# A hybrid decoder layer on one core: softmax scalings and a convolution step moved to ScalarE, norms of the last product by ScalarE, third tile by an accumulating store

## The chip, the cores and the metric

The kernel runs on one core of a Trainium2 chip. A core has a matrix engine (PE, TensorE), three engines for elementwise work (DVE = VectorE, ACT = ScalarE, POOL = GpSimd) and a queue engine, SP, that mainly issues transfers (DMAs). Each engine has its own queue of instructions, which it works through strictly in order; semaphores order the engines among each other. Transfers are issued from SP, from ACT and from POOL. The metric is the device time of one execution in microseconds (us), the median over several runs. The profile is of one execution.

## The reference

One layer of a hybrid decoder on 1,024 tokens of width 1,024, with 16 learned tokens put in front (1,040 rows), everything in 32-bit floating point:

```python
u = rmsnorm(h, g_pre_mix)
q, k, v, xr, yr = split(u @ w_in)                 # 512, 128, 128, 512, 512 columns
attn = sliding_window_attention_with_sinks(q, k, v, sinks)   # 8 heads of 64, 2 KV heads
xr = causal_depthwise_conv(xr, conv_w, conv_b)    # width 4
hr = rg_lru(xr, w_a, b_a, w_x, b_x, lru_lambda)   # sigmoid gates, exp, sqrt, scan over time
rec = gelu(yr) * hr
h = h + rmsnorm(concat(attn, rec) @ w_out, g_post_mix)
u = rmsnorm(h, g_pre_ffn)
f = square(relu(u @ w_ff1)) @ w_ff2               # 4096 hidden columns
return (h + rmsnorm(f, g_post_ffn))[16:]
```

An rmsnorm divides each row by the root of its mean square plus 1e-6 and multiplies by a gain per column. The softmax divides by the sum of the exponentials and of exp(sink - maximum).

## The kernel before, in words

**Matrix products.** A 32-bit operand is split into a rounded high part and the remainder (`split`, lines 93 to 100: a cast on ACT at line 95, a subtraction on DVE at line 98), and each product is three matmuls (`mm3`, lines 122 to 125: high by high, high by low, low by high). Both feed-forward products are done with seven half-size products in place of eight (a Strassen scheme), so sums of weight blocks and of activation blocks are made on the way, on DVE (`combine`, line 788) or by an accumulating DMA, which adds what it loads to what is there and is issued by POOL.

**Buffers.** Nearly all tiles come from rings named by tag: "raw" 2 slots, "ws" 4, "a" 16, "b" 17, "c" 8, "d" 4, "e" 2. A slot is given to a new tile when all that read the old tile is done, so a tag also settles when a load may start.

**Order.** The program is written stage by stage; a scheduler of the tile framework, which uses its own model of the machine's times, orders the instructions of each engine. Hand-made order edges come on top: `lut` (line 81) chains all table functions of ACT in the order in which they are written, and `behind` puts DVE work behind a given instruction.

**Stages**, with the times of the profiled execution: loading, norm and transposes to about 24 us. Attention to about 230 us: for four head pairs and two halves `scores` computes the scores, takes maxima (line 467, DVE), exponentials (Exp, ACT), reciprocals of the sums and scales the eight 128x256 blocks by them (line 480, DVE); `attend`, one group later, transposes the scaled blocks on PE (line 495), splits them and multiplies with the values. Between groups PE gets "fills": the projections of queries, of the recurrent branch and of its gate. A projected recurrent chunk goes through `conv` (first step at line 530: multiply by the last tap and add the bias; three more steps on DVE). Then, to about 285 us, the gates (sigmoids), decay and recurrence (Exp, Tanh, Sqrt, a scan on DVE, line 650), the Gelus (`rec_out`), and the output projection (`out_mm`, eight slices of its contraction; the first four, from attention, don't need the recurrent branch). ACT works through the sigmoids, four Exp/Tanh and two Sqrt groups and eight Gelus, for which it loads another function table each time, and through casts of w_out slices among them. Then the first feed-forward product to about 580 us and the second to 964 us, in seven passes `(i, q)` of eight steps each.

**The second product.** `fetch_2` loads the weights of a step four to six steps ahead: a first operand, and for most steps a second one, either by an accumulating DMA or into a slot of its own, which `combine` then adds or subtracts. Tags alternate between "raw" and "e"; for the last pass `LASTW` lists them. `evict` adds the passes' results into accumulators. Output tiles 4 to 7 are complete after pass 5 (`finish_early`), tiles 0 to 3 after pass 6: `finish_half` takes the sum of squares of the columns that are done, `finish_late` the rest. The rows of `out` hold h already. Tiles 0 and 1 (and 4 to 7) are added to it by an accumulating store of POOL; for tiles 2 and 3 h is loaded back (line 1143 and after), added on DVE (line 1177), and stored by SP and ACT, half each (line 1180). The factor of a norm is the power -1/2 of mean square plus 1e-6, computed by POOL (`rstd_of`, line 164; line 1173).

Of the kernel before, what the change touches and what calls it, by code (L numbers as in the profile page):

```python
# [9 lines left out]
F32 = mybir.dt.float32  # L10
F32R = mybir.dt.float32r
AF = mybir.ActivationFunctionType
ALU = mybir.AluOpType
# [3 lines left out]
P = 128  # L17
# [10 lines left out]
EPS = 1e-6  # L28
# [9 lines left out]
def hybrid_layer(  # L38
# [6 lines left out]
    nc = tc.nc  # L45
# [109 lines left out]
    def rstd_of(ssq_parts, n=P):  # L155
        ms = small.tile([P, 1], F32, name="ms", tag="ms")
        if len(ssq_parts) == 1:
            nc.gpsimd.tensor_scalar(ms[:n], ssq_parts[0], EPS, None, op0=ALU.add)
        else:
            nc.vector.scalar_tensor_tensor(  # L160
                ms[:n], ssq_parts[0], EPS, ssq_parts[1], op0=ALU.add, op1=ALU.add
            )
        rs = small.tile([P, 1], F32, name="rs", tag="rs")
        nc.gpsimd.tensor_tensor(rs[:n], ms[:n], half_pow[:n], op=ALU.pow)  # L164
        return rs[:n]


# [264 lines left out]
    def scores(j, half, q):  # L432
        sn = [slot("c", [P, 4, 257]) for _ in range(2)]
        negm = small.tile([P, 2, 4], F32, name="negm", tag="negm")
        den = small.tile([P, 2, 4], F32, name="den", tag="den")
        rden = small.tile([P, 2, 4], F32, name="rden", tag="rden")
        for h in range(2):
            nc.vector.tensor_copy(
                sn[h][:, :, 256], nsink[:, j + 4 * h : j + 4 * h + 1].to_broadcast([P, 4])
            )  # L440
        for bp in range(2):
            for h in range(2):
                sp_ = bank("s", (P, 2, 256))

                def qk(dst, b, hi, lo):
                    c = slice(b * P, (b + 1) * P)
                    nc.tensor.matmul(
                        dst, q[h][:, c], hi, start=True, stop=False,
                        skip_group_check=True,
                    )  # L450
                    nc.tensor.matmul(
                        dst, q[h][:, c], lo, start=False, stop=True,
                        skip_group_check=True,
                    )

                for i in range(2):
                    b = 4 * half + 2 * bp + i
                    if b == 0:
                        qk(sp_[:, i, 0:P], b, km[:, h, :], km[:, 2 + h, :])
                        qk(sp_[:, i, P:256], b, khh[h][:, 0:P], kl[h][:, 0:P])  # L460
                    else:
                        c = slice((b - 1) * P, (b + 1) * P)
                        qk(sp_[:, i, :], b, khh[h][:, c], kl[h][:, c])
                for i in range(2):
                    b = 4 * half + 2 * bp + i
                    k = 2 * bp + i
                    nc.vector.tensor_tensor_reduce(
                        out=sn[h][:, k, 0:256], in0=sp_[:, i, :],
                        in1=mask1 if b == 0 else mask, scale=-1.0,
                        scalar=nsink[:, j + 4 * h : j + 4 * h + 1],  # L470
                        op0=ALU.add, op1=ALU.min, accum_out=negm[:, h, k : k + 1],
                    )
                    lut(
                        sn[h][:, k, :], sn[h][:, k, :], AF.Exp, scale=-1.0,
                        bias=negm[:, h, k : k + 1], accum_out=den[:, h, k : k + 1],
                    )
        for h in range(2):
            nc.vector.reciprocal(rden[:, h, :], den[:, h, :])
            for k in range(4):
                nc.vector.tensor_scalar(  # L480
                    sn[h][:, k, 0:256], sn[h][:, k, 0:256], rden[:, h, k : k + 1],
                    None, op0=ALU.mult,
                )
        return sn

    def attend(j, half, sn):
# [40 lines left out]

    def conv(c, xr, tag="d"):
        y = slot(tag, [P, TT])
        nc.vector.tensor_scalar(  # L530
            y, xr, prm[:, c, 3:4], prm[:, c, 4:5], op0=ALU.mult, op1=ALU.add
        )
        for k in (2, 1, 0):
            s = 3 - k
            nc.vector.scalar_tensor_tensor(
                y[:, s:], xr[:, : TT - s], prm[:, c, k : k + 1], y[:, s:],
                op0=ALU.mult, op1=ALU.add,
            )
        xc[c] = y
# [247 lines left out]
    def combine(dst, x0, x1, op):  # L787
        return nc.vector.tensor_tensor(dst, x0, x1, op=op).ins  # L788
# [113 lines left out]
    for t in range(8):  # L902
# [12 lines left out]
        if t == 6:  # L915
            b21 = operand(u2f[0][2:4])
            hl = slot("b", ESH, F32R), slot("e", ESH, F32R)
            a11_early.update(early(0, 2, hl))

    for p in range(2):  # L920
        p1(p, a11_early[p])
    for p in range(2):
# [93 lines left out]
    def product_by_parts(acc, w, op):  # L1016
# [22 lines left out]


    LASTW = [
        ("raw", None), ("e", "raw"), ("b", None), ("b", None), ("raw", "e"), ("b", None),
        ("e", "raw"), ("b", None),
    ]

    def fetch_2(n):
        i, q = steps[n]
        wx = PLAN[i][1]
        tags = (("raw", "e"), ("e", "raw"))[n % 2] if i < 6 else LASTW[q]
        raws = []  # L1050
        for (a, b), tag in zip(wx[:2], tags):
            if len(wx) == 3 and wx[2] is ADD and raws and (
                q % 3 < 2 if i < 6 else tag is None
            ):
                nc.gpsimd.dma_start(raws[0], w2v[q, a, b], accum_op=ADD)
                break
            r = slot(tag, [P, 2, 512])
            nc.sync.dma_start(r, w2v[q, a, b])
            raws.append(r)
        return raws  # L1060
# [24 lines left out]
    w_low = [None]  # L1085
# [29 lines left out]
    def squares(sq, src, n):  # L1115
        p_ = small.tile([P, 1], F32, name=f"sq{n}", tag=f"sq{n}")
        nc.scalar.activation(sq, src, AF.Square, scale=RMS_SC, accum_out=p_)
        return p_

    def finish_early(j):  # L1120
        acc = facc["1", j]
        o = slot("a", [P, D])
        ssq = [squares(o[:, c], acc[:, c], n) for n, c in enumerate(COLS)]
        nc.vector.scalar_tensor_tensor(
            o, acc, rstd_of(ssq), gffn_b, op0=ALU.mult, op1=ALU.mult
        )
        t = 4 + j
        nc.gpsimd.dma_start(out[t * P : (t + 1) * P, :], o, accum_op=ALU.add)
# [3 lines left out]
    def finish_half(j):  # L1132

        o = slot("a", [P, D])
        acc, c = facc["0", j], COLS[1]
        ssq = small.tile([P, 1], F32, name=f"late{j}", tag=f"late{j}", bufs=1)
        nc.scalar.activation(
            o[:, c], acc[:, c], AF.Square, scale=RMS_SC, accum_out=ssq
        )
        h = None  # L1140
        if j > 1:
            h = slot("d", [P, D])
            nc.sync.dma_start(h, out[j * P : (j + 1) * P, :])
            nc.gpsimd.tensor_scalar(ssq, ssq, EPS, None, op0=ALU.add)
            behind(w_low[0], combine(o[:, c], acc[:, c], gffn_b[:, c], ALU.mult))
        halves[j] = h, o, ssq

    def finish_late(j, y, parts):

        h, o, ssq = halves[j]  # L1150
        acc = facc["0", j]
        for k, c in enumerate(parts):
            yield k
            ins = combine(acc[:, c], y[k], acc[:, c], ALU.add)
            if k == 1:
                behind(w_low[0], ins)
            if j < 2:
                w_low[0] = nc.vector.scalar_tensor_tensor(
                    o, acc, rstd_of([squares(o[:, c], acc[:, c], 0), ssq]), gffn_b,
                    op0=ALU.mult, op1=ALU.mult,  # L1160
                ).ins.name
                nc.gpsimd.dma_start(out[j * P : (j + 1) * P, :], o, accum_op=ALU.add)
                continue
            part = small.tile([P, 1], F32, name=f"part{k}", tag=f"part{k}")
            nc.vector.tensor_tensor_reduce(
                out=o[:, c], in0=acc[:, c], in1=acc[:, c], scale=RMS_SC * RMS_SC,
                scalar=ssq, op0=ALU.mult, op1=ALU.add, accum_out=part,
            )
            ssq = part
        if j < 2:  # L1170
            return
        rs = small.tile([P, 1], F32, name="rs", tag="rs")
        nc.gpsimd.tensor_tensor(rs, ssq, half_pow, op=ALU.pow)
        c = COLS[0]
        combine(o[:, c], acc[:, c], gffn_b[:, c], ALU.mult)
        for c, eng in zip(COLS[::-1], (nc.sync, nc.scalar)):
            w_low[0] = nc.vector.scalar_tensor_tensor(
                o[:, c], o[:, c], rs, h[:, c], op0=ALU.mult, op1=ALU.add
            ).ins.name
            eng.dma_start(out[j * P : (j + 1) * P, c], o[:, c])  # L1180
# [101 lines left out]
```

## Time and profile before

| | |
|---|---|
| median of 3 runs | 974.02 us (973.7 to 976.03) |
| profiled execution: time, span | 972.95 us, 971.1 us |
| PE busy, first to last matmul | 953.7 us, 5.8 to 964.0 us |
| DVE, ACT, POOL busy | 674.6, 502.0, 82.4 us |
| DMA, mean rate | 134 GB/s |
| granted clock of PE | 0.999 |
| DVE scaling 128x256 (L480), ACT Exp 128x257 | 0.350, 0.506 us |
| ACT cast 128x1024 (L95), DVE subtraction 128x1024 (L98) | 1.05, 1.22 us |
| ACT table load | 1.283 us each, 6 at L82 |
| POOL's pow, 128x1 (L164, L1173) | 0.57 (median of the late ones), 0.99 us |
| accumulating stores (L1162, L1128), issue to landing | 5.0 to 5.1, 6.5 to 9.8 us |
| plain half-tile stores (L1180), issue to landing | 2.1 to 2.6 us |

A busy time is the sum of an engine's instructions; successive instructions of ACT and DVE overlap by about 0.1 us, so what a series takes is less than the sum of its durations. For a single instruction the duration counts, for a series the distance from start to start. Matmuls of 512 columns start 0.23 us apart, those of 256 columns 0.12. In a timeline line the first number is the start, the second the duration, then engine, line of the code, operation, the tile written and the tiles read, and in brackets how long the engine stood idle before and what ended that.

### The profile page before, as it was taken

The numbers are of one execution on the slowest core, as the hardware profiler recorded it, in microseconds if no ns is written. First come the engines' busy times: TensorE is split into PE (matmuls) and PEld (weight loads), VectorE is DVE, ScalarE is ACT, GpSimd is POOL, SyncE is SP. The second block draws the span as 40 slices with busy tenths as digits, with TensorE's granted clock in tenths as the row PEclk, the third lists the DMA queues.
The fourth block names the chain that finished last, engine by engine and source line by source line (L and its number), as shares of the span: only waits on it lengthen the run. The fifth ranks groups of instructions, "written<-read, shape, count | busy, mean of one in ns | idle before, by whom it ended". The sixth has DMA issues, their size and how long they took to land.

```text
span 971.1 us, 12490 instructions
## 1 busy us (share of the span) xinstructions
PE 953.7 (98%) x4782; PEld 803.0 (83%) x4782; DVE 674.6 (69%) x997; ACT 502.0 (52%) x809; POOL 82.4 (8%) x109
## 2 busy tenths in 40 slices
PE   6999999999999999999999999999999999999997
PEld 6999999888878887888888878888888888888786
DVE  6679997775976686665645465468557676779694
ACT  6646673567844554343555556555433344445350
POOL 4100000000002100000000000000111000003152
PEclk9999999999999999999999999999999999999999
DMA  9002001012234466576522264323678765548923
GB/s 296 23 1 66 23 23 44 23 48 64 84 119 144 159 207 209 173 251 209 198 87 87 97 206 125 114 87 114 172 176 198 186 224 187 184 163 195 223 80 87
DMA packets 88219, 130.13 MB, mean 134 GB/s; under 512 B 13624, under 2 KB 52552, under 8 KB 88160
## 3 DMA queue, kind: packets, MB, share of 16 engines
q1 hardware_dynamic: 79792, 107.33, 33.4%
q0 software_dynamic: 7792, 20.45, 10.1%
q10 hardware_dynamic: 576, 1.57, 0.4%
q8 instruction: 37, 0.61, 0.2%
q14 instruction: 22, 0.18, 0.1%
HBM read 110.46 MB, written 18.87 MB: 133 GB/s over the span
## 4 chain that ended last, share of the span: by engine, by line
PE 89%; DVE 4%; DMA 3%; issue 2%; ACT 1%; POOL 0%; SPq 0%; POOLq 0%; DVEq 0%; ACTq 0%
PE ps_acc L124 11%; PE ps_acc L123 11%; PE ps_acc L125 11%; PE ps_s L125 6%; PE ps_pt L123 6%; PE ps_s L124 6%; PE ps_pt L125 6%; PE ps_s L123 6%; PE ps_pt L124 6%; PE ps_o L124 5%; PE ps_o L123 5%; PE ps_o L125 5%; PE ps_o L506 2%; PE ps_pt L495 1%; DMA raw<-in_w_ff_dram 1%
## 5 line engine op out<-in xcount | busy, mean ns | idle before, releaser
L95 ACT CAST ws<-raw 128x1024 fp32r<-128x1024 f32 (+1 forms) x69 | 70.7, 1024 | 126.6 <-PE ps_o L124 48.8
L98 DVE TENSOR_TENSOR ws<-raw,ws 128x1024 fp32r<-128x1024 f32 (+1 forms) x70 | 83.5, 1194 | 59.6 <-ACT ws L95 59.5
L123 PE MATMUL ps_acc<-a,ws 128*128 128x256 f32 (+2 forms) x272 | 90.5, 333 | 0.6 <-DVE b L305 0.6
L124 PE MATMUL ps_acc<-a,ws 128*128 128x256 f32 (+2 forms) x272 | 89.8, 330 | 0.0
L125 PE MATMUL ps_acc<-a,ws 128*128 128x256 f32 (+2 forms) x272 | 89.4, 329 | 0.0
L98 DVE TENSOR_TENSOR b<-b,b 128x1024 fp32r<-128x1024 f32 (+2 forms) x48 | 57.6, 1201 | 24.7 <-PE ps_o L124 17.1
L95 ACT CAST ws<-e 128x1024 fp32r<-128x1024 f32 x43 | 45.0, 1046 | 55.3 <-PE ps_o L124 28.1
L95 ACT CAST b<-b 128x1024 fp32r<-128x1024 f32 (+2 forms) x48 | 49.4, 1030 | 42.8 <-DVE b L788 40.0
L98 DVE TENSOR_TENSOR ws<-e,ws 128x1024 fp32r<-128x1024 f32 x43 | 52.6, 1222 | 21.6 <-ACT ws L95 21.6
L123 PEld LDWEIGHTS ps_acc<-a,ws 128*128 128x128 f32 x272 | 51.2, 188 | 4.9 <-DVE b L305 0.8
L125 PEld LDWEIGHTS ps_acc<-a,ws 128*128 128x128 f32 x272 | 51.2, 188 | 4.6
L124 PEld LDWEIGHTS ps_acc<-a,ws 128*128 128x128 f32 x272 | 51.2, 188 | 3.9
L164 POOL TENSOR_TENSOR rs<-ms,half_pow 128x1 f32<-128x1 f32 (+1 forms) x31 | 21.3, 692 | 356.5 <-DVE ms L160 355.1
L123 PE MATMUL ps_acc<-ws,b 128*128 128x512 f32 (+1 forms) x120 | 46.3, 386 | 0.4 <-ACT ws L95 0.4
L124 PE MATMUL ps_acc<-ws,b 128*128 128x512 f32 (+1 forms) x120 | 46.5, 388 | 0.2 <-DVE ws L98 0.2
L125 PE MATMUL ps_acc<-ws,b 128*128 128x512 f32 (+1 forms) x120 | 46.2, 385 | 0.0
L123 PE MATMUL ps_pt<-ws,b 128*128 128x512 f32 x112 | 44.1, 394 | 0.0
L124 PE MATMUL ps_pt<-ws,b 128*128 128x512 f32 x112 | 44.1, 394 | 0.0
L125 PE MATMUL ps_pt<-ws,b 128*128 128x512 f32 x112 | 44.0, 393 | 0.0
L123 PE MATMUL ps_s<-ws,b 128*128 128x512 f32 x110 | 43.4, 395 | 0.0
L124 PE MATMUL ps_s<-ws,b 128*128 128x512 f32 x110 | 43.3, 393 | 0.0
L125 PE MATMUL ps_s<-ws,b 128*128 128x512 f32 x110 | 43.3, 393 | 0.0
(381 smaller groups left out, 2690.1 us busy)
## 6 DMA issues: line engine op xcount, KB each, us to landing
raw<-in_w_ff_dram SPq DMA_DIRECT2D x62, 512.0 KB, 4.0
e<-in_w_ff_dram SPq DMA_DIRECT2D x45, 512.0 KB, 3.6
d<-in_w_ff_dram SPq DMA_DIRECT2D x12, 512.0 KB, 3.8
s_dram<-d POOLq DMA_DIRECT2D x12, 512.0 KB, 3.9
raw<-in_w_in_dram SPq DMA_DIRECT2D x9, 512.0 KB, 3.6
c<-in_x_dram SPq DMA_DIRECT2D x8, 512.0 KB, 8.5
d<-in_x_dram SPq DMA_DIRECT2D x8, 512.0 KB, 4.6
out_dram<-raw SPq DMA_DIRECT2D x8, 512.0 KB, 2.6
```

Of the source, the lines that this page charges most:

```text
L95: nc.scalar.copy(hi, src)
L98: low = nc.vector.tensor_tensor(lo, src, f32(hi), op=ALU.subtract).ins
L123: nc.tensor.matmul(dst, lh, rh, start=start, stop=False, skip_group_check=True)
L124: nc.tensor.matmul(dst, lh, rl, start=False, stop=False, skip_group_check=True)
L125: nc.tensor.matmul(dst, ll, rh, start=False, stop=stop, skip_group_check=True)
L164: nc.gpsimd.tensor_tensor(rs[:n], ms[:n], half_pow[:n], op=ALU.pow)
L495: nc.tensor.transpose(pt[:, o : o + P], sn[h][:, 2 * bp + i, s * P : (s + 1) * P], ident,)
L506: nc.tensor.matmul(po[:, oc : oc + n], v, p_[:, pc : pc + n], start=first and k == 0, stop=last and k == 1, skip_group_check=True,)
```

## The change

1. `scores`: of the four scalings of each head, the second and fourth become an ACT copy with a scale per row; the first and third stay on DVE.
2. `conv`: the first step becomes an ACT Identity with scale and bias per row.
3. `load_root`, called after the output projection's loop is written and ahead of the first feed-forward product, computes one Sqrt of a 128x1 column, so that ACT's table for Sqrt is loaded there. It goes through `lut`, and thereby follows the Gelus.
4. `finish_early`, `finish_half`, `finish_late`: the norm's factor is made by `root_rstd`, a Sqrt on ACT with the other part of the mean square as its bias and a reciprocal on DVE, in place of POOL's power; the 1e-6 is added by an ACT Identity. For the last tile the one with k = 1 follows the second reduction, and the multiplication by the gain is done in two halves.
5. The third output tile (j = 2) is finished as the first two: one 128x1024 multiply and an accumulating store by POOL. Its h isn't loaded back, and its two plain stores are gone.
6. `fetch_2`: in passes 2 to 5 (i > 1) a second operand that has a slot of its own goes to an "a" slot; in the last pass, the first weights go to a "b" slot in place of "raw".

```diff
+    def load_root():
+        root = small.tile([P, 1], F32, name="root", tag="root")
+        lut(root, eps_col, AF.Sqrt)
+
+    def root_rstd(ssq, bias, n=P):
+        sd = small.tile([P, 1], F32, name="sd", tag="sd")
+        lut(sd[:n], ssq, AF.Sqrt, bias=bias)
+        rs = small.tile([P, 1], F32, name="rs", tag="rs")
+        nc.vector.reciprocal(rs[:n], sd[:n])
         return rs[:n]
...
             for k in range(4):
-                nc.vector.tensor_scalar(
-                    sn[h][:, k, 0:256], sn[h][:, k, 0:256], rden[:, h, k : k + 1],
-                    None, op0=ALU.mult,
-                )
+                p_, r_ = sn[h][:, k, 0:256], rden[:, h, k : k + 1]
+                if k % 2:
+                    nc.scalar.activation(p_, p_, AF.Copy, scale=r_)
+                else:
+                    nc.vector.tensor_scalar(p_, p_, r_, None, op0=ALU.mult)
...
     def conv(c, xr, tag="d"):
-        nc.vector.tensor_scalar(
-            y, xr, prm[:, c, 3:4], prm[:, c, 4:5], op0=ALU.mult, op1=ALU.add
+        nc.scalar.activation(
+            y, xr, AF.Identity, scale=prm[:, c, 3:4], bias=prm[:, c, 4:5]
         )
...
+    load_root()
     for p in range(2):
         p1(p, a11_early[p])
...
     LASTW = [
-        ("raw", None), ("e", "raw"), ("b", None), ("b", None), ("raw", "e"), ("b", None),
+        ("b", None), ("e", "raw"), ("b", None), ("b", None), ("raw", "e"), ("b", None),
...
     def fetch_2(n):
-        tags = (("raw", "e"), ("e", "raw"))[n % 2] if i < 6 else LASTW[q]
+        tags = LASTW[q]
+        if i < 6:
+            tags = ("raw", "e")[n % 2], "a" if i > 1 else ("e", "raw")[n % 2]
...
     def finish_early(j):
+        nc.scalar.activation(ssq[0], ssq[0], AF.Identity, bias=eps_col)
+        rs = root_rstd(ssq[1], ssq[0])
         nc.vector.scalar_tensor_tensor(
-            o, acc, rstd_of(ssq), gffn_b, op0=ALU.mult, op1=ALU.mult
+            o, acc, rs, gffn_b, op0=ALU.mult, op1=ALU.mult
         )
...
     def finish_half(j):
+        nc.scalar.activation(ssq, ssq, AF.Identity, bias=eps_col)
         h = None
-        if j > 1:
+        if j > 2:
             h = slot("d", [P, D])
             nc.sync.dma_start(h, out[j * P : (j + 1) * P, :])
-            nc.gpsimd.tensor_scalar(ssq, ssq, EPS, None, op0=ALU.add)
...
     def finish_late(j, y, parts):
-            if j < 2:
+            if j < 3:
                 w_low[0] = nc.vector.scalar_tensor_tensor(
-                    o, acc, rstd_of([squares(o[:, c], acc[:, c], 0), ssq]), gffn_b,
+                    o, acc, root_rstd(squares(o[:, c], acc[:, c], 0), ssq), gffn_b,
...
             ssq = part
-        if j < 2:
+            if k == 1:
+                rs = root_rstd(ssq, 0.0)
+            w_low[0] = combine(o[:, c], acc[:, c], gffn_b[:, c], ALU.mult).name
+        if j < 3:
             return
-        rs = small.tile([P, 1], F32, name="rs", tag="rs")
-        nc.gpsimd.tensor_tensor(rs, ssq, half_pow, op=ALU.pow)
-        c = COLS[0]
-        combine(o[:, c], acc[:, c], gffn_b[:, c], ALU.mult)
```

More of the change, by code (lines that the diff above doesn't have):

```diff
@@ L164, in rstd_of @@
         nc.gpsimd.tensor_tensor(rs[:n], ms[:n], half_pow[:n], op=ALU.pow)
+        return rs[:n]
+    eps_col = const.tile([P, 1], F32, name="eps_col")
+    nc.gpsimd.memset(eps_col, EPS)
+    def load_root():
[6 more added lines that the diff above has]
+        nc.vector.reciprocal(rs[:n], sd[:n])
         return rs[:n]
```

## The prediction

> **What bounds the kernel now.** I read the page's first part and its chain that ended last, then busy time by stage, then the timelines at the few places where TensorE (PE) stands still. The page, parts 1 and 4:
>
> ```profile
> PE 953.7 (98%) x4782; PEld 803.0 (83%) x4782; DVE 674.6 (69%) x997; ACT 502.0 (52%) x809; POOL 82.4 (8%) x109
> ...
> PE 89%; DVE 4%; DMA 3%; issue 2%; ACT 1%; POOL 0%; SPq 0%; POOLq 0%; DVEq 0%; ACTq 0%
> ```
>
> PE is the bound: 953.7 of 971.1 us, at a granted clock of 0.999. The change takes no matmul away, so it can gain only in the 17.4 us in which PE is idle, and it loses wherever it makes PE wait. Busy time by stage (window, then PE, weight loads, DVE, ACT, POOL, clock, DMA share, GB/s), for attention (three rows) and gates to output projection:
>
> ```profile
> 60.00:120.00 60.00, 60.00 (x444) 56.72 (x443) 54.58 (x152) 38.13 (x102) 0.00 (x0) 1.00 0.14 36
> 120.00:180.00 60.00, 60.00 (x429) 56.21 (x428) 47.61 (x109) 33.09 (x81) 0.00 (x0) 1.00 0.11 33
> 180.00:230.00 50.00, 50.00 (x284) 44.24 (x283) 36.24 (x77) 30.05 (x63) 0.00 (x0) 1.00 0.13 37
> 230.00:270.00 40.00, 40.00 (x180) 32.95 (x179) 30.41 (x27) 34.19 (x40) 0.00 (x0) 1.00 0.24 78
> ```
>
> No row has any PE idle time: there is nothing to win in attention, where half of the edits lie. ACT has 69 us free in the first three rows, but only 5.8 of 40 in the last. PE stops after its start in five places: 364 us (0.84, untouched by the change), 578 (0.22, untouched), and these, from PE's timeline:
>
> ```profile
> 271.82 0.73 PE L123 MATMUL ps_pt<-a,b 128*128 128x512 f32 x2 [0.41 <-ACT b L95]
> 918.05 0.50 PE L123 MATMUL ps_acc<-ws,b 128*128 128x512 f32 x1 [0.40 <-ACT ws L95]
> 919.31 0.50 PE L124 MATMUL ps_acc<-ws,b 128*128 128x512 f32 x1 [0.18 <-DVE ws L98]
> ```
>
> Counted from start to start against the usual 0.23 us, they cost 0.56, 0.57 and 0.34 us. The rest is the tail, 7.1 us after PE's last matmul ends at 964.0.
>
> **The change part by part.** The sum runs against the profiled execution: span 971.1 us, time 972.95 us. It is 1.07 us below the median of the runs (974.02); I carry the difference over to the median.
>
> *Attention scalings and convolution step.* DVE loses 32 scalings at 0.262 us (four in 1.13 us) and four 128x1040 steps at 0.82, 11.7 us. ACT gains 32 scalings; the nearest row is the 128x256 activation with a scale per partition (L116, 0.483 us, about 0.39 start to start), so 12.5 us, and four steps at 1.07 (the 128x1040 exponential's pitch), 4.3 us. ACT goes from 101.3 to about 118 of 170 us. The cover is the projection fills that keep PE at 60.00 of 60.00; without it each group of eight scalings lies between its Exps and PE's transposes. The eight of a group now run on two queues (about 1.6 us for 2.1) but a scaling may stand behind one 128x1024 cast of ACT (1.05 us). Ends: 0, since PE has no idle to give back, and 2 us, a quarter of a cast in each of eight groups. I take 0, the nearest row being PE's full windows.
>
> *Gates to output projection.* Here the order of the program changes, and ACT is the queue that matters. ACT's timeline before:
>
> ```profile
> 233.88 0.55 ACT L82 ACTIVATE c<-ps_o,prm 128x344 f32<-128x344 f32 x1
> 234.45 1.28 ACT L82 ACT_TABLE_LOAD   x1
> ...
> 256.72 0.64 ACT L82 ACTIVATE d<-d 128x512 f32<-128x512 f32 x1
> ...
> 260.90 1.03 ACT L95 CAST a<-d 128x1024 fp32r<-128x1024 f32 x1
> 261.84 0.62 ACT L95 CAST b<-d 128x512 fp32r<-128x512 f32 x1
> 262.36 0.62 ACT L95 CAST b<-b 128x512 fp32r<-128x512 f32 x1
> ```
>
> The cast at 261.84 rounds the first recurrent output; PE's first matmul with it is at 265.01, where the 96 matmuls that cover this stretch (out-projection over the first four slices, 22.2 us) run out. Its slack is 265.01 - 262.46 = 2.55 us. In the changed order: (1) the last gate matmul stands eight fill matmuls of 512 columns later, and the last sigmoid starts about 2.07 us later; (2) five w_out casts, not three, stand between the sigmoids and the Gelus, 2 x 0.95 = 1.90; (3) after the Gelus come the table load for Sqrt, 1.28 us, and a one-column Sqrt, 0.15 (nearest row 0.167, the 64x16 cast); (4) then one w_out cast, 0.95, where before also one stood. So first Gelu at 260.7, last done about 264.9, table and root to 266.3, w_out cast to 267.3, the wanted cast done at 267.9. The DVE chain beside it, by its durations, delivers the product at 264.7, and the w_out slice for the first of these casts is loaded by 260, so ACT sets the time. PE waits 267.9 - 265.0 = 2.9 us. Behind that the deadlines are met: the low half of this operand, at 270.4, is first read 16 matmuls (3.7 us) on, at 271.6; the next chunk is ready at 275.6 and read at 278.3. So the gap at 271 is not there again: +2.9 - 0.6 = **+2.3 us**. Ends: -0.6 (delays of 5.4 us are 2.5 too many; if two of the four vanish there is no wait) and +3.5 (the gap stays and all ends late).
>
> For step 3 the row is the table load's: all six loads before take 1,283 ns each, with 0.1 us of idle ahead of all six together, so a switch costs 1.3 us. The Trainium skill (ScalarE: Activation LUTs, section What ACT_TABLE_LOAD costs) gives the same 1283 ns but adds a drain of about 1380 ns to every switch; the load at 234.45 starts 0.02 us behind the sigmoid's end, and the exponential follows at 235.74, so this trace shows no drain. By the page the wait would be 4.3 us and the time 976.2 us, which stays within 0.3%; as far as the traces bear it out I give it 0.03, inside the forecast's share.
>
> *Second feed-forward product: loads.* The first weights of the last pass move from a "raw" to a "b" slot, and 18 second operands to "a" slots. From the chain before:
>
> ```profile
> 907.68 9.19 DMA raw<-in_w_ff_dram
> ...
> 916.96 1.05 ACT ws L95
> ```
>
> The accumulating load was issued at 907.68, on POOL behind another accumulating load (901.75) and the fourth early output store (902.51), landed at 916.9, and PE waited 0.57 + 0.34. Now SP's plain load needs only its b slot (free at the end of a pass-five step, about 895.9; landed about 901.7), and POOL's accumulation is issued ahead of the last two early stores, landing by about 911.5 even at 9.2 us. The cast is then held by its ws slot until 912.5, enough: **-0.9 us**; ends -0.9 and 0. The "a" loads keep their place in SP's queue, with waits on DVE combines done long before; POOL loses eight pow and two additions and gains one store; SP loses one load and one store. All this is beside PE at 599.26 of 600 us (300 to 900); if a load came late, the cost would be a gap like the 0.9 of before.
>
> *Norms and third tile.* In the early tiles ACT takes a bias addition and a Sqrt (0.2 to 0.3 us each), DVE a reciprocal (0.17, the 128x4 row): nobody waits but an output store, so zero, hidden by the last pass. In the tail, DVE's order before is
>
> ```profile
> 959.79 0.69 DVE L788 TENSOR_TENSOR a<-ps_pt,a 128x512 f32<-128x512 f32 x1 [0.49 <-PE ps_pt L125]
> ...
> 962.46 1.42 DVE L1177 SCALAR_TENSOR_TENSOR a<-a,rs,d 128x512 f32<-128x512 f32 x2
> ...
> 966.31 1.41 DVE L1177 SCALAR_TENSOR_TENSOR a<-a,rs,d 128x512 f32<-128x512 f32 x2 [0.44 <-POOL rs L1173]
> ```
>
> For the third tile ACT squares (0.63 + 0.19) to 961.3 and roots to 961.6; its single 128x1024 multiply (1.28) runs 962.3 to 963.55, 0.24 earlier than the pair before. The fourth tile's two reductions and combines then end at 965.2; Sqrt 0.25 and reciprocal 0.17 in place of POOL's pow (0.99 + 0.1) give the final pair at 965.7 instead of 966.3: **-0.6 us**, ends -0.8 and 0. The third tile's store is now POOL's: issued 0.7 us behind the multiply (as 959.98 is behind 959.29), at 964.25, and landing 5.1 us later (L1162's rows) at 969.35, half a microsecond ahead of the fourth tile's last store (967.25 + 2.6 = 969.85).
>
> Sum: 0 + 2.3 - 0.9 - 0.6 = +0.8 us, 973.8 on the profiled execution, **974.8 us** on the median.
>
> **The rivals.** *A: ACT becomes the bound in attention* (slower). Place: the transposes behind a group's scalings. Speaking for it: a scaling can queue behind a 1.05 us cast, and a few of PE's waits there are met with under 0.1 us to spare. Against: 52 us free on ACT, PE full. It decides once PE loses 2.1 us in all, 0.26 per group: 977 to 979 us. *B: no wait at 265* (faster than before, though hardly beyond what can be measured): if the casts and the table load find ACT free earlier, because the sigmoids are not really two microseconds later. Then -0.6 - 0.9 - 0.6 = -2.1: 971.9 us. *C: the third tile's store ends the program.* The other accumulating stores (L1128) took 6.5 to 9.8 us to land; at 7.5 the end is 1.9 us later, 976.7, at 9.8, 4.2 later, 979.0. Against: both of the last stores before took 5.0 to 5.1, with DMA nearly idle as now. *D: the load change does nothing*, since another transfer is late: 975.7.
>
> **How the numbers follow.** Runs of this kernel span 973.7 to 976.03, so a difference under 0.3% (2.9 us) can't be told from none. Forecast (D within it, 0.05) 0.55; B 0.15; A 0.22; C 0.08. Even B stays inside 2.9 us; faster by more takes B with something that no row shows, such as the 0.84 us at 364: 0.09. Slower: nearly all of A and half of C, and some of the forecast where the wait is 5 us: 0.29. The remaining 0.62 is within 0.3%. The range, from below B to A with C's smaller price: 971.5 to 978.5.
>
> **What the changed profile would show.** Right: PE waits once about 3 us near 265 for ACT's cast, the gap near 271 gone; six table loads until then and a seventh just behind the Gelus; PE full at 60 to 230; no gap at the start of the last pass; the fourth tile's final pair 1.7 us behind PE's end, not 2.3. Wrong: PE idle under 60.00 in the attention rows (A); no wait at 265 (B); the last landing that of POOL's store (C).

## The result

The changed kernel takes 983.08 us (median of six runs, 981.37 to 987.11) against 974.26 us for the kernel before: ratio 1.0094, 95% interval 1.0071 to 1.0117. It is slower by nearly 1%; the forecast was 974.8 us. The profiled execution takes 982.91 us (span 981.0 us), 9.96 us more than that of before. Of all executions in this document one, of the kernel under "Attention back on DVE", took twice as long as its others (1938.66 us against 979.63 to 981.53); its time and its profile are left out.

The page of the changed kernel, part 1:

```profile
PE 954.6 (97%) x4782; PEld 802.4 (82%) x4782; DVE 660.9 (67%) x959; ACT 524.6 (53%) x865; POOL 62.9 (6%) x101
```

PE is busy as long as before in a span that is 9.9 us longer: nearly all of the loss is time in which PE waits. Busy time by stage, in the columns of the prediction's table (window, then PE, weight loads, DVE, ACT, POOL, clock, DMA share, GB/s):

```profile
60.00:120.00 60.00, 60.00 (x445) 56.89 (x445) 49.51 (x137) 47.27 (x121) 0.00 (x0) 1.00 0.15 36
120.00:180.00 60.00, 59.40 (x425) 55.55 (x424) 43.76 (x99) 37.05 (x88) 0.00 (x0) 1.00 0.10 28
180.00:230.00 50.00, 50.00 (x283) 44.16 (x282) 33.94 (x69) 33.36 (x73) 0.00 (x0) 1.00 0.16 43
230.00:270.00 40.00, 37.22 (x168) 30.45 (x167) 28.43 (x26) 35.79 (x43) 0.00 (x0) 1.00 0.27 79
...
580.00:900.00 320.00, 314.55 (x1357) 254.17 (x1356) 213.21 (x206) 149.99 (x170) 16.33 (x14) 1.00 0.55 157
900.00:940.00 40.00, 40.00 (x187) 33.10 (x186) 35.50 (x36) 19.43 (x28) 7.00 (x7) 1.00 0.94 237
```

The rows with a hole are 120 to 180 (0.6 us), 230 to 270 (2.8) and 580 to 900 (5.45). The last is the second feed-forward product, in which the prediction had found PE full and charged nothing. The list of PE's waits (engine and line, what it waited for: us in all, times, longest) names the two large ones, the first for the second product:

```profile
PE ps_acc L124 <- DVE ws L98: 5.4, 5, 1.3
PE ps_pt L123 <- ACT b L95: 2.8, 1, 2.8
```

Counted from start to start of PE's matmuls, before and after (us):

| where | before | after | difference |
|---|---|---|---|
| 27 us, behind the first transposes (no edit there; 25.9 to 28.5 in the profiles of this study) | at 27.19 | at 27.64 | +0.45 |
| attention, 134 us | 0 | 0.77 | +0.77 |
| output projection, 266 to 272 us | 0.56 | 2.95 | +2.39 |
| second product, 717 us | 0 | 1.34 | +1.34 |
| second product, 818, 824, 831, 838 us | 0 | 0.55, 1.40, 1.47, 1.42 | +4.84 |
| second product, 862 us | 0 | 0.23 | +0.23 |
| start of the last pass, 917 and 919 us | 0.57, 0.34 | 0 | -0.91 |
| end of PE's last matmul to the end | 7.1 | 7.8 | +0.7 |

With +0.05 from two small ones (469 and 578 us) that is +9.9 us, as much as the span grew.

**The waits in the second product.** In pass 4 the weights are a difference of two blocks; DVE's timeline of the changed kernel there (start, duration, line, tile written and tiles read, idle before; line 804 is the combine, line 98 with a ws tile the subtraction that makes the low half of the weights):

```profile
809.33 1.23 DVE L804 TENSOR_TENSOR e<-e,a 128x1024 f32<-128x1024 f32 x1 [4.10 <-issue]
810.47 1.22 DVE L98 TENSOR_TENSOR ws<-raw,ws 128x1024 fp32r<-128x1024 f32 x1
811.61 1.22 DVE L98 TENSOR_TENSOR b<-b,b 128x1024 fp32r<-128x1024 f32 x1
816.52 1.23 DVE L804 TENSOR_TENSOR raw<-raw,a 128x1024 f32<-128x1024 f32 x1 [3.69 <-issue]
817.66 1.22 DVE L98 TENSOR_TENSOR ws<-e,ws 128x1024 fp32r<-128x1024 f32 x1
...
823.58 1.23 DVE L804 TENSOR_TENSOR e<-e,a 128x1024 f32<-128x1024 f32 x1 [3.57 <-DMA e<-in_w_ff_dram]
```

and SP's, which issues the loads:

```profile
810.58 0.37 SPq L1077 DMA_DIRECT2D a<-in_w_ff_dram  x1
811.72 0.37 SPq L1077 DMA_DIRECT2D raw<-in_w_ff_dram  x1
817.77 0.37 SPq L1077 DMA_DIRECT2D a<-in_w_ff_dram  x1
818.90 0.37 SPq L1077 DMA_DIRECT2D e<-in_w_ff_dram  x1
```

The combine at 809.33 belongs to a step three ahead of the low half at 810.47 that PE needs now. The low half ends at 811.69; that frees its "raw" slot, and the load into it goes out at 811.72. It is wanted by the combine at 816.52, which stands in DVE's queue ahead of the next low half, 817.66. (In two of the three brackets the profile names no releaser, "issue"; at 823.58 it names the load.) So each step of the loop holds a combine (1.14 to the next start), a low half (1.22) and a load (4.7 to 4.8): 7.1 us, where PE has matmuls for 5.6. DVE is idle for half of it. The second operands' loads hang on the combines too; of SP's list of waits from 800 to 845 us (us in all, times, longest):

```profile
SPq L1077 <- DVE e L804: 20.0, 4, 6.6
SPq L1077 <- DVE raw L804: 12.5, 3, 5.6
```

Before, such waits come to 8.2 us, and the same two kinds of instruction stand the other way round:

```profile
807.48 1.23 DVE L98 TENSOR_TENSOR ws<-e,ws 128x1024 fp32r<-128x1024 f32 x1 [1.66 <-ACT ws L95]
808.62 1.22 DVE L788 TENSOR_TENSOR e<-e,raw 128x1024 f32<-128x1024 f32 x1
```

**The wait at 266.** PE's first matmul with the recurrent output, and ACT's timeline ahead of it:

```profile
269.38 0.50 PE L123 MATMUL ps_pt<-a,b 128*128 128x512 f32 x1 [2.78 <-ACT b L95]
```

```profile
237.38 0.55 ACT L82 ACTIVATE c<-ps_o,prm 128x344 f32<-128x344 f32 x1 [2.01 <-PE ps_o L125]
237.94 1.28 ACT L82 ACT_TABLE_LOAD   x1
...
262.10 0.63 ACT L82 ACTIVATE d<-d 128x512 f32<-128x512 f32 x1
...
265.24 1.13 ACT L82 ACTIVATE d<-d 128x512 f32<-128x512 f32 x2
266.38 1.28 ACT L82 ACT_TABLE_LOAD   x1
267.68 0.20 ACT L82 ACTIVATE root<-eps_col 128x1 f32<-128x1 f32 x1
267.79 1.03 ACT L95 CAST a<-d 128x1024 fp32r<-128x1024 f32 x1
268.72 0.61 ACT L95 CAST b<-d 128x512 fp32r<-128x512 f32 x1
```

The cast at 268.72 is the one that PE waits for. Less the 1.2 us by which PE was late already (0.45 + 0.77), the last sigmoid starts at 236.2 (forecast 235.95, which is 233.88 + 2.07), the first Gelu at 260.9 (260.7), the cast ends at 268.1 (267.9). The chain was read rightly.

**The tail.** The last entries of DVE's timeline, and the stores' landing times by line of the code:

```profile
971.54 1.27 DVE L1179 SCALAR_TENSOR_TENSOR a<-a,rs,a 128x1024 f32<-128x1024 f32 x1
...
975.11 1.42 DVE L1197 SCALAR_TENSOR_TENSOR a<-a,rs,d 128x512 f32<-128x512 f32 x2
```

```profile
DMA to landing us min/median/max: 5.3/5.3/5.5
...
DMA to landing us min/median/max: 3.5/3.5/3.5
```

The upper line is POOL's accumulating stores (L1183), the lower the last plain store of the fourth tile on ACT's queue (L1200). Before, the fourth tile's plain stores took 2.1 us and the third tile's 2.5 and 2.6. DVE is done 3.25 us behind PE's last matmul (973.28), not 3.7 as before, but the end comes 0.7 us later.

### The profile page after: what moved, and what is told of

Read it like the earlier page. It is cut to its first block, busy times and chain, and to the rows that moved or that the text cites. A ratio compares the mean times of both kernels' runs of the same rounds, so it can differ in the third digit from the quotient of the medians.

```text
span 981.0 us, 12473 instructions
## 1 busy us (share of the span) xinstructions
PE 954.6 (97%) x4782; PEld 802.4 (82%) x4782; DVE 660.9 (67%) x959; ACT 524.6 (53%) x865; POOL 62.9 (6%) x101
## 5 line engine op out<-in xcount | busy, mean ns | idle before, releaser
L123 PE MATMUL ps_o<-ws,b 128*128 128x512 f32 (+1 forms) x108 | 41.3, 383 | 0.0
```

The source lines that it names most:

```text
L123: nc.tensor.matmul(dst, lh, rh, start=start, stop=False, skip_group_check=True)
```

## The experiments

Unless said otherwise, ratios are to the kernel before on the same chip, with 95% intervals; where there is no ratio, one execution was profiled. Theory 1 is that the waits of the second product come from DVE's order; its rivals are given with each.

### Second operands back in raw and e

```diff
-        tags = LASTW[q]
-        if i < 6:
-            tags = ("raw", "e")[n % 2], "a" if i > 1 else ("e", "raw")[n % 2]
+        tags = (("raw", "e"), ("e", "raw"))[n % 2] if i < 6 else LASTW[q]
```

> The changed kernel with only the slots of the second operands put back (alternating raw and e, as before; the last pass's first weights stay in b). In the changed kernel PE waited five times, 6.2 us in all, between 717 and 840 us for a low half that DVE makes. Theory 1: with the second operands in a-slots the scheduler puts the combine of the step three ahead in front of the low half of the present step in DVE's queue; that combine waits for a load whose slot the low half before it frees, so one step takes combine 1.14 + low half 1.22 + load 4.8 = 7.1 us instead of PE's 5.6. With the old slots the combine follows the low half again: the gaps go, 6.2 us, and the span is about 974.8. Rival theory 2 (the weights of the last pass in b-slots, or more store traffic, delay these loads): the gaps stay, about 981.

Ratio 1.0036 (1.0021 to 1.0050), 977.48 us. All the waits between 717 and 862 us are gone; the last pass's weights are still in b-slots, so these did not make them. The span is 976.8, not 974.8, and PE's timeline says why:

```profile
267.01 0.40 PE L125 MATMUL ps_s<-a,b 128*128 128x512 f32 x1
270.19 0.80 PE L123 MATMUL ps_pt<-a,b 128*128 128x512 f32 x1 [2.79 <-ACT b L95]
270.79 0.63 PE L124 MATMUL ps_pt<-a,b 128*128 128x512 f32 x1
271.21 0.63 PE L123 MATMUL ps_pt<-a,b 128*128 128x512 f32 x1
```

Behind the wait, which is as long as in the changed kernel, the matmuls start 0.43 us apart in place of 0.23 until 276.3 (the first 0.59): thirteen of them, and 2.9 us. The granted clock is 0.50 from 269.6 to 276.4 us.

### The low half first

```diff
-            if i == 6:
+            if i > 1:
                 behind(w_low[0], ins)
```

> The changed kernel with the a-slots kept and one order edge more: from the third pass on, the combine of a step goes behind the low half of the step before. Matmuls and transfers are the same, only DVE's order differs. Theory 1 (DVE's order): the five gaps between 717 and 862 us go, 6 us, span about 975. Rival theory 2 (the a-slots themselves: two loads at once land later, and SP issues an a-load that waits ahead of the first operand's load): the gaps stay, 1.4 us each, span about 981. Between them, if part of the wait is SP's: 2 to 4 us go.

Ratio 1.0045 (1.0029 to 1.0061), 978.56 us, clear of the changed kernel's 1.0071 to 1.0117. PE's order, the slots and the transfers are those of the changed kernel. DVE's order differs, with it a little of ACT's, and from 789 us SP issues the two loads of a step the other way round (the first operand, then the a-load). That swap is hardly what helps: in the changed kernel the raw load, though second in SP's queue, went out 0.03 us behind the end of the low half that frees its slot (811.69, 811.72). All four waits of pass 4 and that at 862 are gone:

```profile
804.95 1.22 DVE L98 TENSOR_TENSOR ws<-e,ws 128x1024 fp32r<-128x1024 f32 x1 [1.45 <-ACT ws L95]
806.10 1.22 DVE L804 TENSOR_TENSOR raw<-raw,a 128x1024 f32<-128x1024 f32 x1
```

The low half comes first, neither of the two waits for a load, and a step takes 5.5 us. Of the wait at 717, 0.91 us stays, and this execution has 1.8 us of waits at 471 to 473 us, in a stage that the edit leaves as it was (0.27 there in the changed kernel's profile). In pass 4 the a-slots as such cost nothing; theory 1 holds there. At 717 it is another chain: the combine ahead of the low half waits there for the last second operand that still has a raw slot, and in the changed kernel that load goes out 5.6 us later than before (708.78, 703.15) where PE by then is 4.5 us later. What holds it back was not tested.

### The a-slots alone in the kernel before

```diff
-        tags = (("raw", "e"), ("e", "raw"))[n % 2] if i < 6 else LASTW[q]
+        tags = LASTW[q]
+        if i < 6:
+            tags = ("raw", "e")[n % 2], "a" if i > 1 else ("e", "raw")[n % 2]
```

> The kernel before with only the second operands of passes 2 to 5 in a-slots. Theory 1: DVE's order again has the combine ahead by three steps, so the gaps come alone, 1.4 us each in pass 4: slower by about 6 us, 980 us. Rival: the gaps need the rest of the change (ACT's extra work, the b-slot): no change, 974 us.

Ratio 1.0046 (1.0028 to 1.0064), 978.67 us. Four waits (712, 819, 825 and 832 us: 0.89, 0.43, 1.53, 1.51), 4.4 us in all. The edit makes them by itself, and DVE's timeline has the combine ahead of the low half again (824.32 and 825.46); the forecast of 6 was high by a third.

### No Sqrt behind the Gelus

```diff
-    load_root()
+    pass
```

> The changed kernel without the one-column Sqrt after the Gelus and so without its table load there (the table is loaded at the first norm of the second product instead). In the changed kernel PE waits 2.95 us at 266. By the prediction's sum the load and the Sqrt are 1.4 us of that: the wait becomes 1.5 us and the span 1.4 us shorter, 979.6. Rival: DVE's queue, whose low half of the w_out slice comes later too, sets the next wait, and the time stays within 0.5 us of the changed kernel's.

Ratio 1.0055 (1.0037 to 1.0073), 979.81 us. The wait at 266 is 1.45 us, 1.5 less, as the sum has it, and the rival's next wait does not come. The profiled span is 979.1 us, 1.9 less than the changed kernel's: 1.5 of it are this wait, and the waits of the second product are not shorter (6.7 us here, 6.4 there).

### Attention back on DVE, and each half of it

```diff
-                if k % 2:
+                if False:
...
-        nc.scalar.activation(
-            y, xr, AF.Identity, scale=prm[:, c, 3:4], bias=prm[:, c, 4:5]
-        )
+        nc.vector.tensor_scalar(
+            y, xr, prm[:, c, 3:4], prm[:, c, 4:5], op0=ALU.mult, op1=ALU.add
+        )
```

> The changed kernel with the softmax scalings and the first convolution step put back on DVE; all else as changed. The prediction charged nothing to attention itself but 4 us of the delay at 266 to what follows from it (last sigmoid 2.07 us later, two w_out casts more ahead of the Gelus, 1.90). If that is right, the gap at 134 us (0.77) goes and the wait at 266 falls by more than 2 us, from 2.95 to under 1: span about 3 us shorter than the changed kernel's, 978, with no stretch of slow clock behind the wait. Rival: the scheduler puts the casts there because of the table load, not because of ACT's load in attention; then the wait stays above 2.5 us and only the 0.8 goes.

Ratio 1.0079 (1.0063 to 1.0094); the interval meets the changed kernel's (1.0071 to 1.0117), so the timed runs alone don't show a gain. The kernel was profiled once more:

> The kernel of attention_on_dve once more, for a profile at full clock (the profile of the first was taken in an execution at half clock). Its timed runs lie about 1.5 us under the changed kernel's. By the prediction's sum (sigmoids 2.07 us earlier, two casts behind the Gelus again) the wait at 266 falls from 2.95 to under 1 us and the gap at 134 us is gone, 2.8 us; for the timed difference to be 1.5, something else has to be 1 us worse, most likely the gaps between 717 and 840 us, which have no reason to stay the same. Rival: the wait at 266 is still above 2 us.

Span 976.3 us. No wait at 134; at 267 and 272 two waits of 0.70 us each in place of the one of 2.95. So 0.77 + 1.55 us belong to this edit. The waits of the second product are there as in the changed kernel, 4.8 us in this execution. With the first hunk of this diff undone (scalings on ACT, convolution on DVE):

> The changed kernel with the first convolution step back on DVE, the scalings left on ACT. The planned order still has the two w_out casts ahead of the Gelus. If the scalings alone make the delay, the wait at 266 is 2 to 3 us and the gap at 134 is there or not according to whether the convolution step (1.1 us of ACT) makes it: it is not there if the convolution step stands in ACT's queue ahead of the rounding of a query projection, and is there if scalings do. Rival: the convolution makes the delay; then the wait is under 1 us.

Span 978.0. The wait at 265 is 2.95 us, with the two w_out casts ahead of the Gelus; the one at 134 is gone, but one of 0.84 stands at 156, for a copy on ACT (line 354). With the second hunk undone (convolution on ACT, scalings on DVE):

> The changed kernel with the scalings back on DVE, the convolution step left on ACT. The planned order has the two w_out casts behind the Gelus, as in the kernel before. If the scalings make the delay at 266, the wait there is 1 us or less (the Sqrt load alone: 1.4 + the sigmoids' shift, if any, minus 2.55 of slack, so 0 to 0.9). Rival: above 2 us.

Span 975.0. Two waits of 0.70 us at 266 and 271, and none in attention. By these profiles, one execution each, the scalings make the delay and the wait in attention, though not always at the same place; the convolution step alone costs nothing that they show.

### The third tile by plain stores

```diff
-        if j > 2:
+        if j > 1:
             h = slot("d", [P, D])
...
-            if j < 3:
+            if j < 2:
...
-            if k == 1:
+            if k == len(parts) - 1:
                 rs = root_rstd(ssq, 0.0)
...
-        if j < 3:
+        if j < 2:
             return
```

> The changed kernel with the third tile finished as before, by h loaded back and two plain stores, its norm still by ScalarE. In the changed kernel the program ends 7.7 us behind PE's last matmul, 7.1 before, though DVE is done 0.5 us earlier than before: the last two plain stores take 3.5 us to land instead of 2.6. Theory: they share the DMA engines with the third tile's accumulating store, issued 2.5 us ahead of them. Then the plain stores land in about 2.6 us again and the end comes 6.6 to 6.8 us behind PE's last matmul, 1 us less. Rival: the plain stores are slower for another reason (no change, 7.7), or the scalar chain of the third tile costs on DVE what the store saves (7.2).

The program ends 6.8 us behind PE's last matmul (975.69), 1.0 less than in the changed kernel. The fourth tile's stores, with no accumulating store ahead, take 2.1 us to land, the third tile's, issued 3.3 and 4.0 us behind an accumulating one, 2.6 and 2.7. So the accumulating store costs 1.0 us in the profile; that it does so by slowing the plain ones behind it fits, but how it slows them was not tested. The span, 982.5 us, is longer all the same, for 3.1 us of waits at 459 to 473 us, a stage that the edit leaves as it was. In the timed runs nothing of it can be seen: 1.0105 (1.0089 to 1.0121) beside the changed kernel's 1.0094 (1.0071 to 1.0117).

### A longer wait

```diff
+    pad = const.tile([P, 1], F32, name="pad")
...
+    for _ in range(7):
+        lut(pad, eps_col, AF.Gelu_apprx_tanh)
     for c in range(NLRU):
         rec_out(c, 0)
```

on the kernel with second operands in raw and e.

> The changed kernel with the old slots for the second operands (no gaps in the second product), and seven more one-column table functions on ACT ahead of the Gelus, so that the wait at 266 us grows from 2.95 to about 5 us (1.4 of it by these, 0.95 by a w_out cast that the scheduler moves ahead). With a wait of 2.95 us one profile showed full clock afterwards and two showed 7 and 13 matmuls of 512 columns 0.427 us apart in place of 0.231 (0.196 each). Theory: a long enough wait of PE lowers the granted clock, 2.95 us is at the edge. Then every matmul for at least 3 us behind the longer wait is 0.427 us apart, 13 or more of them, 2.5 us on top of the wait; span 976.8 + 2.1 = 979. Rival: the slow matmuls come from something else in that run; then none or as few as before, and the slow stretch is not longer.

The wait is 5.25 us. By stretches, in the columns of the first table:

```profile
266.00:271.00 5.00, 0.30 (x2) 0.00 (x0) 5.00 (x5) 4.98 (x9) 0.00 (x0) 0.72 0.34 107
271.00:275.00 4.00, 3.62 (x9) 2.86 (x10) 4.00 (x4) 0.85 (x2) 0.00 (x0) 0.50 0.00 0
```

The span is 976.9 us, 2 less than expected. The clock falls at 268.2, while PE waits, and stays at 0.50 until 275.1: the first matmul takes 0.59 us to the next, seven more 0.43, 1.8 us lost in all. That is fewer than the thirteen that I had named, and the shorter wait of 2.95 us was once followed by more. The clock is low for 6.8 us here as it is in second_raw_e, but nearly half of that falls into the wait: the loss does not grow with the wait. The last section says on what it depends.

### The b-slot alone in the kernel before

```diff
     LASTW = [
-        ("raw", None), ("e", "raw"), ("b", None), ("b", None), ("raw", "e"), ("b", None),
+        ("b", None), ("e", "raw"), ("b", None), ("b", None), ("raw", "e"), ("b", None),
```

> The kernel before with only the first weights of the last pass in a b-slot. Prediction: the two gaps at 917 and 919 us (0.57 and 0.34) go and nothing else moves: 0.9 us faster, ratio 0.9991. Rival: the fetch in the b-slot displaces another load, and the gap stays or comes elsewhere: no difference.

Ratio 1.0040 (1.0025 to 1.0054), 977.36 us: slower, where the prediction's own step says 0.9 us faster. The waits at 917 and 919 us are gone, but PE waits 4.95 us at 902, with six slow matmuls behind it. (The profile also has 0.5 us at 739 and 1.55 at 774; the latter is in both_best below as well.) POOL's timeline, and DVE's:

```profile
893.06 1.21 POOL L1055 DMA_DIRECT2D b<-in_w_ff_dram  x1 [1.43 <-issue]
903.04 1.22 POOL L1055 DMA_DIRECT2D b<-in_w_ff_dram  x1 [8.77 <-issue]
903.80 1.05 POOL L164 TENSOR_TENSOR rs<-ms,half_pow 128x1 f32<-128x1 f32 x1
```

```profile
904.88 1.28 DVE L1124 SCALAR_TENSOR_TENSOR a<-b,rs,a 128x1024 f32<-128x1024 f32 x1 [8.96 <-POOL rs L164]
906.09 1.22 DVE L98 TENSOR_TENSOR ws<-e,ws 128x1024 fp32r<-128x1024 f32 x1
```

In this order a second accumulating load stands in POOL's queue ahead of the power for the fourth early tile; in the kernel before the power came first, at 893.19, and that load at 901.75. Here the load is issued only at 903.04, the power comes 0.76 us behind, the multiply by it blocks DVE for 9 us, and the low half behind that multiply is what PE waits for. In the changed kernel the norms need no power of POOL, so nothing of DVE's hangs on that queue.

### What is left without the parts that cost

The changed kernel with all of the above put back: second operands in raw and e, no Sqrt behind the Gelus, scalings and convolution on DVE, third tile by plain stores. Kept are the norms by ScalarE and the b-slot.

> What is left of the change without the parts that cost: second operands in raw and e, no Sqrt after the Gelus, scalings and convolution on DVE, third tile by plain stores; kept are the last pass's first weights in a b-slot and the norms by ScalarE. If the parts add up, the order up to the second product is that of the kernel before, the gaps at 917 and 919 us go (-0.9), the tail is 0.3 to 0.5 us shorter, and the wait at 271 (0.56) stays: span about 969.8, ratio 0.9986. Rival: the table load that moves into the second product, or the norms' extra work on ACT in the last pass, gives it back: 971.

Ratio 0.9977 (0.9963 to 0.9991), median 971.53 us against 973.58: faster than both kernels. The page and the tail: span 970.8 us, no waits at 902 to 919, and 6.8 us from PE's last matmul to the end (7.1 before). The profiled execution has a wait of 1.76 us at 774, where DVE waited 4.6 us for a weight load; without it the span would be some 969, the forecast being 969.8.

## Why the prediction was wrong, point by point

- *Bound, and attention.* That nothing was to be gained in attention held. The charge of 0 did not: 0.8 us, within its bounds (0 to 2) and, by one profile each, from the scalings. In the changed kernel PE waits at 134 us for the low half of a query projection (line 117).
- *Gates to output projection.* Forecast +2.3, measured +2.4; the wait 2.9 against 2.95. The four delays were rightly read: taking the load of the table and its Sqrt away took 1.5 us off, forecast 1.43; leaving the scalings on DVE brought the two casts behind the Gelus again, and what was left was 1.4 us in two waits. What the sum lacked is that a wait of this length can lower the clock. No term of it was for that.
- *Second product: loads.* Here the prediction failed. The step reads: "The "a" loads keep their place in SP's queue, with waits on DVE combines done long before", and it charged 0. I looked at who releases the loads and at SP's order, and not at what new slots let the scheduler do with DVE's order. In the changed kernel the combine of the step three ahead stands in front of the low half that PE needs, and DVE's queue waits for loads; with more first operands in flight the scheduler has room for that, but why it chose so was not tested. The combines are not done long before either: from 800 to 845 us SP's loads wait 32.5 us for them, 8.2 before. Measured: 6.4 us in the changed kernel and 4.4 as the only edit; even for a late load the step named no more than "a gap like the 0.9 of before". low_half_first shows the order to be the cause in pass 4; of the wait at 717 it leaves 0.9 us, whose cause stays open. Without the 6.4 us the profiled time would be 976.5, inside the range.
- *The b-slot.* -0.9 came out as forecast, at the places named. But the step gave it to the slot alone; alone it costs 0.4%. The number came out because another edit takes POOL's powers away: the step counted them among what is "beside PE" and did not say that its own gain hangs on them.
- *Tail.* DVE's part came out: -0.5, forecast -0.6. The landing of the last plain store did not: 3.5 us in place of 2.6. The 2.6 was the third tile's row of before, for stores issued behind an accumulating one; the fourth tile's, alone, took 2.1. So the forecast of the end mixed two cases, and the new case, an accumulating store 3.2 us ahead, cost more than either. Rival C had the store itself landing last; it lands at about 978.8, before the plain one.
- *Rivals and range.* A's time (977 to 979), with C's upper price (979.0), was closest, but A's mechanism makes 0.8 us of the 9.9. No rival had DVE's order in the second product in it, and the range ended 4.6 us too low.

## What to carry to other kernels

When buffers are added or a tag is changed, compare the order of the engine that consumes the loads, not only the releases of the slots: an instruction that waits for a load must not stand ahead of the one that the bound engine needs next. A term that is read from the profile of before holds with the company that it had there (a store alone on the queues, a POOL queue with or without a power in it); when several edits touch the same queue, price them together. On a PE-bound kernel a wait of three microseconds can cost up to twice its length: 2.95 us cost 2.9 more in one profile and nothing more in three.

## What the runs showed of the hardware that was not expected

**The clock behind a wait of PE.** Of five profiles with a wait of 2.95 us at the same place, three show full clock behind it and two show 0.50, with seven and thirteen matmuls of 512 columns 0.427 us apart (1.6 and 2.9 us lost). With 4.95 us (b_slot_alone) there are six, with 5.25 seven, each time behind a first one of 0.59; with waits up to 2.1 us (only_scalings at 715) there are none. Of the ten runs of second_raw_e, two at a mean clock of 0.994 take 978.8 and 978.9 us and two at 0.999 take 975.1 and 975.9, but the slowest, 980.5, has 0.997, so the clock is not all that varies. The Trainium skill (TensorE: Matmul & The Clock Gate, section Part 1: The HAM clock gate) says that the array falls to half its clock after an idle window of about 3.4 us, that the window runs freely, and that slow stretches vary from run to run. The halving, the free-running window and the variation agree with these traces; the length does not quite: 2.95 us from start to start were enough twice.

What decides can be read off the traces. The granted clock changes only at the edges of windows of 3.413 us that run on whatever PE does: in b_slot_alone it is 0.50 from 907.24 to 910.66, one window, and falls again at 972.10, 18 windows on; in second_raw_e it is 0.50 from 269.56 to 276.38, two windows. Busy time in three such windows (second_raw_e, longer_wait, only_scalings):

```profile
266.15:269.56 3.41, 1.26 (x6) 0.69 (x4) 3.41 (x5) 3.39 (x6) 0.00 (x0) 1.00 0.00 0
264.83:268.24 3.41, 1.47 (x7) 0.85 (x5) 3.41 (x5) 3.41 (x7) 0.00 (x0) 1.00 0.49 155
266.24:269.65 3.41, 1.63 (x7) 1.36 (x8) 3.41 (x3) 3.19 (x6) 0.00 (x0) 1.00 0.00 0
```

Behind the first two the clock falls, behind the third it does not. The same holds in all thirteen profiles for every window at full clock, from the clock's first rise to its fall behind PE's last matmul: the clock was halved behind each window with 1.51 us of PE or less, and behind none with 1.62 or more. It came back behind windows with 3.30 us of PE or more, not behind one with 2.78, which is why second_raw_e lost two windows. So a wait of 2.95 us costs its length alone where an edge divides it near the middle (1.86 and 2.19 us of PE on the two sides in the changed kernel's profile) and more where one window takes most of it. Which of the two happens is luck in each execution.

**The switch of a function table.** The load at 266.38 starts 0.01 us behind the last Gelu and the Sqrt follows 1.30 us after its start. That is again 1.3 us and not the 2.66 that the Trainium skill (ScalarE: Activation LUTs, section What ACT_TABLE_LOAD costs) gives with its drain; the wait that it made, 1.5 us with the Sqrt, agrees with the row.

**Plain stores beside an accumulating one.** The fourth tile's last half store (256 KB) takes 3.5 us to land with a 512 KB accumulating store issued 3.2 us ahead of it in the changed kernel. The third tile's, 3.3 to 4.0 us behind such a store, take 2.5 to 2.7 (before, third_plain, both_best), and the fourth tile's with none in flight 2.0 to 2.1. Why 3.2 and 3.3 us differ so much, no run shows.
